# One decoder layer on one Trainium2 core: cell transposes placed later, gathered steps moved from the mixer to the dense pass, own rings for the attention's doubled halves

## Chip, cores and metric

The kernel runs on one core of one Trainium2 chip. The metric is the time of one execution on the device, in microseconds (us); each kernel is given by the median of its runs.

## What is computed

One layer of a hybrid decoder for 1024 tokens of width 1024 (batch 1), in float32. Cut to what matters:

```python
h = rms_norm(x); q, k, v, mq, mk, mv, mo, mi, mf = split(h @ w_in)
# group A: differential attention, 4 heads, two score maps of 64 columns each, ALiBi, causal
pr = softmax(q @ k.T * 64**-0.5 - slope * dist)            # for c in 0, 1
da = rms_norm((pr[0] - lam * pr[1]) @ v) * (1 - lambda_init)
# group B: mLSTM, 4 heads: causal conv and silu on mq and mk, a scan over chunks of 64 tokens
ml = rms_norm(sigmoid(mo) * mlstm_chunkwise(mq, mk, mv, mi, mf))
x += concat(da, ml) @ w_out
# PEER: 8 heads; per token and head the best 16 of 128 x 128 experts by product keys
q = (rms_norm(x) @ w_query).reshape(8, 2, 128)
eidx, g = top_k of the sums of the two halves' scores, softmax over the 16
x += sum_k g[k] * gelu(rms_norm(x) . expert_u[eidx[k]]) * expert_v[eidx[k]]
x += sigmoid(rms_norm(x) @ w_ple_gate) * (p @ w_ple_proj)
return rms_norm(x)
```

## The kernel before

**Stages.** `front(part)` runs for two parts of 512 tokens: the mixer (attention and mLSTM), the output projection (`wout`, eight weights), the query projection (`wq`, sixteen weights) and the choice of the experts. Then come `dense_up` and `dense_down` over 128 tables of the expert matrices each, and `tail` (the gate and the final norm) over eight tiles of 128 tokens. Every large product is done in three fp32r matmuls of high and low parts (`mm3s`), so each weight is loaded (`wraw`), copied to `whi` on ScalarE and subtracted to `wlo` on VectorE; a table likewise to `thi` (L841) and `tlo` (L842).

**Dense and gathered tiles.** Five of the eight token tiles go through all experts densely. The other three (tiles 0, 1, 2) gather their experts: `sparse` yields 400 steps, and a step gathers (but for the first and last sixteen, which have one half of it) one row of `expert_u` per token (`ru`, GpSimd's indirect DMA at L788, used on VectorE at L804) and one row of `expert_v` (`rv`, used at L822, which adds to `ya`). When the last step of a tile is done, `ya` is stored, and `tail` loads it again; tile 2 is the last of the tail's order `TORD`. `pump(rate)` pulls steps: before each projection, each output weight and each query weight of part 1 by `F_RATE`, before each table of `dense_up` by `UP_RATE` (the first rate up to the table given as third number, the second from there), each group of four tables of `dense_down` by `DOWN_RATE`, and in the tail. The first fourteen or so pulls in part 1 are the second top-k. The gathered rows land in a ring of `NR` buffers.

**The order of the work.** The kernel is written as generators that are stepped in turn; a scheduler fixes the order on every engine when the kernel is built, by the order of the code, the tiles' rings and priorities (a pulled step is put 800 places ahead, and `anchor` and `behind` keep a gathered instruction behind the last weight's split). On the chip each engine works off its own list.

**A head of the mixer.** `qkv(h)` projects queries, keys and values (three pieces). It takes `qT` from PSUM (L371), and `queries` and `keys` call `doubled`, which copies each half of the partitions twice by SyncE's DMAs (L260), and from these copies form `qab` and `kab`, the high and low parts for the scores `S` (L411). In part 1 the keys of part 0 come back from `kt_s`. `attention(h)` has six pieces: five steps over its query tiles, and a last one with the norm's `ro` chain (`rsqrt`, L116 to L125, on VectorE, four numbers per partition), the copies of `by_tile` (L364, ScalarE), the output's transposes (L448, TensorE) and `mixed`. `ml_inputs(h)` and `mlstm(h)` project and run the cell; the cell's last piece transposes its output (L558). `qT`, `kT`, the doubled halves, the attention's output `osb` and others share a ring `t2` of eight buffers of 512 columns (`T2`). The mixed tiles go to `mx_s` and are loaded again at the end of the mixer (L584 to L590).

**Queues.** SyncE's queue (SPq) holds weights, tables, doubled halves and mixed tiles in one order; GpSimd issues the gathers.

## Time and profile before

| | us |
|---|---|
| median of three runs (3212.78 to 3213.87) | 3213.16 |
| the profiled execution | 3213.83 |
| its span in the trace | 3212.0 |
| TensorE (PE) busy | 2954.8 (92%) |
| VectorE (DVE) busy | 2521.5 (79%) |
| ScalarE (ACT) busy | 1160.2 (36%) |
| GpSimd (POOL) busy | 1013.0 (32%) |
| DMA | 829.53 MB, 258 GB/s in the mean |

The stages lie in the span like this: part 0 to 465 us, part 1's mixer to 860, its output and query projections to 950, its top-k to 1065, the dense up pass to 2170, the dense down pass to 3075, and the tail to 3212. The busy times are means over these stages; a stage is read by its own stretch. A row of the stretches gives the length, the busy time of each engine with the number of its instructions, TensorE's granted clock (1.00 is the full one), the mean busy share of the 16 DMA engines and their rate.

### The profile page before, as it was taken

The numbers are of one execution on the slowest core, as the hardware profiler recorded it, in microseconds if no ns is written. First come the engines' busy times: TensorE is split into PE (matmuls) and PEld (weight loads), VectorE is DVE, ScalarE is ACT, GpSimd is POOL, SyncE is SP. The second block draws the span as 40 slices with busy tenths as digits, with TensorE's granted clock in tenths as the row PEclk, the third lists the DMA queues.
The fourth block names the chain that finished last, engine by engine and source line by source line (L and its number), as shares of the span: only waits on it lengthen the run. The fifth ranks groups of instructions, "written<-read, shape, count | busy, mean of one in ns | idle before, by whom it ended". The sixth has DMA issues, their size and how long they took to land.

```text
span 3212.0 us, 44687 instructions
## 1 busy us (share of the span) xinstructions
PE 2954.8 (92%) x16367; PEld 2601.1 (81%) x16367; DVE 2521.5 (79%) x5381; ACT 1160.2 (36%) x1994; POOL 1013.0 (32%) x786
## 2 busy tenths in 40 slices
PE   7998889887579799999999999988989999999987
PEld 6776767676467799999999999977878888887866
DVE  5564689888889999978766667557878888888786
ACT  5664335554322232245343433322222222222233
POOL 0000000344541544412433334343333444442330
PEclk9998989998789899999999999989999999999999
DMA  5333433678874788876888878899989999998762
GB/s 163 96 107 108 143 120 95 232 234 274 323 264 147 290 317 313 284 262 244 329 314 299 293 278 311 313 343 343 327 316 337 334 334 331 334 327 286 265 209 92
DMA packets 317148, 829.53 MB, mean 258 GB/s; under 512 B 26240, under 2 KB 115200, under 8 KB 314368
## 3 DMA queue, kind: packets, MB, share of 16 engines
q0 software_dynamic: 112608, 410.04, 36.2%
q1 hardware_dynamic: 185888, 374.68, 33.8%
q10 hardware_dynamic: 18432, 41.95, 3.5%
q8 instruction: 128, 2.10, 0.3%
q14 instruction: 92, 0.75, 0.1%
HBM read 715.95 MB, written 102.24 MB: 255 GB/s over the span
## 4 chain that ended last, share of the span: by engine, by line
PE 53%; DVE 19%; issue 14%; DMA 8%; POOL 4%; ACT 2%; SPq 0%; POOLq 0%; DVEq 0%; ACTq 0%
PE A L143 16%; PE mm L143 10%; PE keep L143 6%; DVE ya L822 3%; PE S L143 3%; DVE ru L804 2%; DMA rv<-in_ev,eidx 2%; PE Y L135 2%; PE Y L134 2%; PE Y L136 2%; DMA raw<-in_vr 2%; POOL rv L788 2%; PE pg L894 2%; PE pg L895 2%; DVE tlo L842 2%
## 5 line engine op out<-in xcount | busy, mean ns | idle before, releaser
L788 POOL DMA_INDIRECT ru<-in_eu,eidx x384 | 507.5, 1321 | 1201.8 <-DVE ru L804 845.1
L788 POOL DMA_INDIRECT rv<-in_ev,eidx x384 | 497.5, 1296 | 442.6 <-DVE ya L822 300.7
L842 DVE TENSOR_TENSOR tlo<-raw,thi 128x1024 fp32r<-128x1024 f32 x256 | 312.9, 1222 | 299.1 <-issue 168.5
L822 DVE SCALAR_TENSOR_TENSOR ya<-rv,cf,ya 128x1024 f32<-128x1024 f32 x384 | 492.8, 1283 | 40.3 <-DMA rv<-in_ev,eidx 28.1
L841 ACT ACTIVATE thi<-raw 128x1024 fp32r<-128x1024 f32 x256 | 268.0, 1058 | 683.4 <-PE A L143 380.8
L804 DVE SCALAR_TENSOR_TENSOR ru<-ru,sh 128x1024 f32<-128x1024 f32 x384 | 468.8, 1221 | 20.8 <-DMA ru<-in_eu,eidx 19.6
L143 PE MATMUL A<-ahi,thi 128*128 128x384 f32 x1024 | 348.7, 341 | 4.3 <-ACT ga L954 4.3
L143 PE MATMUL A<-alo,thi 128*128 128x384 f32 x1024 | 346.6, 338 | 0.0
L143 PE MATMUL mm<-ahi,whi 128*128 128x512 f32 (+1 forms) x752 | 299.7, 402 | 22.2 <-ACT ahi L234 12.4
L143 PE MATMUL mm<-alo,whi 128*128 128x512 f32 (+1 forms) x752 | 286.2, 393 | 7.1 <-DVE alo L235 7.1
L134 PE MATMUL Y<-thi,ph 128*128 128x512 f32 x640 | 250.3, 391 | 6.6 <-ACT thi L841 4.8
L143 PE MATMUL A<-xh,thi 128*128 128x256 f32 x1024 | 250.8, 283 | 0.7 <-ACT xh L933 0.7
L143 PE MATMUL A<-xl,thi 128*128 128x256 f32 x1024 | 250.6, 282 | 0.1
L135 PE MATMUL Y<-tlo,ph 128*128 128x512 f32 x640 | 249.8, 390 | 0.5 <-DVE tlo L842 0.5
L136 PE MATMUL Y<-thi,pl 128*128 128x512 f32 x640 | 249.5, 390 | 0.0
L143 PE MATMUL A<-ahi,tlo 128*128 128x384 f32 x1024 | 202.7, 338 | 13.8 <-DVE tlo L842 13.7
L1021 ACT ACTIVATE ph<-aq 128x640 fp32r<-128x640 f32 x128 | 87.5, 729 | 330.8 <-PE Y L135 325.3
L143 PEld LDWEIGHTS A<-ahi,thi 128*128 128x128 f32 x1024 | 195.1, 191 | 4.5 <-ACT ga L954 4.5
L143 PE MATMUL mm<-ahi,wlo 128*128 128x512 f32 (+1 forms) x752 | 193.7, 388 | 5.5 <-DVE wlo L194 5.5
L143 PEld LDWEIGHTS A<-xh,thi 128*128 128x128 f32 x1024 | 195.0, 190 | 1.0 <-ACT xh L933 0.9
L143 PEld LDWEIGHTS A<-xl,thi 128*128 128x128 f32 x1024 | 194.8, 190 | 0.3 <-DVE xl L934 0.3
L143 PEld LDWEIGHTS A<-alo,thi 128*128 128x128 f32 x1024 | 195.0, 190 | 0.0
(462 smaller groups left out, 6160.0 us busy)
## 6 DMA issues: line engine op xcount, KB each, us to landing
raw<-in_ut SPq DMA_DIRECT2D x128, 512.0 KB, 5.9
raw<-in_vr SPq DMA_DIRECT2D x128, 512.0 KB, 5.5
ga_s<-ga ACTq DMA_DIRECT2D x128, 320.0 KB, 5.6
g_s<-st SPq DMA_DIRECT2D x20, 2048.0 KB, 8.3
gq<-g_s SPq DMA_DIRECT2D x32, 1280.0 KB, 10.8
aq<-ga_s SPq DMA_DIRECT2D x32, 1280.0 KB, 8.7
wraw<-in_win SPq DMA_DIRECT2D x58, 512.0 KB, 3.4
wraw<-in_wq SPq DMA_DIRECT2D x32, 512.0 KB, 3.7
```

The costliest lines, as they stand in the source:

```text
L134: pe.matmul(o, lh, rh, start=start, stop=False)
L135: pe.matmul(o, lh, rl, start=False, stop=False)
L136: pe.matmul(o, ll, rh, start=False, stop=stop)
L143: pe.matmul(o, ll if p == "l" else lh, rl if p == "r" else rh, start=start and p == "h", stop=stop and n == last and p == names[-1])
L788: gp.indirect_dma_start(out=b, out_offset=None, in_=table, in_offset=bass.IndirectOffsetOnAxis(ap=eidx[part][:, i, k:k + 1], axis=0))
L804: behind(v.scalar_tensor_tensor(b, b, 1.0, st["h", tl], op0=OP.mult, op1=OP.mult, accum_out=st["d", n][:, j:j + 1]))
L822: op = v.scalar_tensor_tensor(ya, b, st["c", n][:, j:j + 1], ya, op0=OP.mult, op1=OP.add)
L841: sc.activation(hi, raw, AF.Copy)
L842: anchor(v.tensor_sub(lo, raw, hi.bitcast(F32)))
L894: pe.matmul(pg[:, b, :], o0[:, a, :, b], w0[:, a, :, b], start=True, stop=False)
L895: pe.matmul(pg[:, b, :], o0[:, a, :, b], w1[:, a, :, b], start=False, stop=True)
L1021: sc.activation(ph, av, AF.Copy)
```

## The change

The constants: `NR` 4 to 3 for the ring of gathered rows in the front, and a ring of its own with `NRU = 4` for `dense_up`; the doubled halves get a ring `dd` of two, `qT` and `kT` a ring `qk` of two, in place of `t2`, which stays at eight. The pump rates of the front fall, those of `dense_up` change, those of `dense_down` and the tail stay. In the mixer's loop the generators are stepped in another order; `attention` yields six times, so a seventh step of it does nothing.

```diff
-NR = 4
+NR = 3
+NRU = 4
+NDD = 2
...
-F_RATE = (2.4, 1.6, 2.0)
-UP_RATE = (1.0, 1.2, 56)
+F_RATE = (1.8, 1.3, 1.5)
+UP_RATE = (0.9, 1.45, 40)
 DOWN_RATE = 1.05
...
                 def doubled(src, c):
-                    d = pa.tile([P, T], F32, name="t2", bufs=T2)
+                    d = pa.tile([P, T], F32, name="dd", bufs=NDD)
...
-                    qT = pa.tile([P, T], F32, name="t2", bufs=T2)
+                    qT = pa.tile([P, T], F32, name="qk", bufs=2)
...
-                    kT = pa.tile([P, T], F32, name="t2", bufs=T2)
+                    kT = pa.tile([P, T], F32, name="qk", bufs=2)
...
                     att, inputs = attention(h), ml_inputs(h)
-                    step(att, cell)
-                    for _ in range(4):
+                    step(att)
+                    step(inputs, cell, att)
+                    for _ in range(3):
                         step(inputs, att)
-                    step(att)
                     cell = mlstm(h)
                     nxt = qkv(h + 1) if h + 1 < H else None
-                    for _ in range(3):
-                        step(cell, nxt)
+                    step(att, cell, nxt, cell, nxt, att, cell, nxt)
                 step(cell)
...
     front(0, ptk)
-    ring["pool"] = rstk.enter_context(pool("rg", side="right"))
+    fring = ExitStack()
+    ring["pool"] = fring.enter_context(pool("rg", side="right"))
     ring["bufs"] = NR
...
     fstk.close()
+    fring.close()
+    ring["pool"] = rstk.enter_context(pool("rgu", side="right"))
+    ring["bufs"] = NRU
     dense_up(ptk)
```

The line numbers of the changed kernel are two higher up to the mixer's loop, and one higher behind it up to `tail`. In the built order three places show the change.

VectorE in part 1, inside the `ro` chain of the last head's attention (`ro_h`, `ro_m` and `ro_u` are the chain's, `ru` and `rv` gathered rows). Before:

```order
L822 SCALAR_TENSOR_TENSOR ya<-rv,cf,ya 128x1024
L123 TENSOR_TENSOR ro_h<-ro_u 128x4
L804 SCALAR_TENSOR_TENSOR ru,dots<-ru,sh_5145 128x1024
L124 TENSOR_TENSOR ro_h<-ro_h,ro_m 128x4
L822 SCALAR_TENSOR_TENSOR ya<-rv,cf,ya 128x1024
L125 SCALAR_TENSOR_TENSOR ro_u<-ro_h,ro_u 128x4
L804 SCALAR_TENSOR_TENSOR ru,dots<-ru,sh_5145 128x1024
L123 TENSOR_TENSOR ro_h<-ro_u 128x4
L822 SCALAR_TENSOR_TENSOR ya<-rv,cf,ya 128x1024
L124 TENSOR_TENSOR ro_h<-ro_h,ro_m 128x4
L804 SCALAR_TENSOR_TENSOR ru,dots<-ru,sh_5145 128x1024
```

After:

```order
L823 SCALAR_TENSOR_TENSOR ya<-rv,cf,ya 128x1024
L125 TENSOR_TENSOR ro_h<-ro_u 128x4
L805 SCALAR_TENSOR_TENSOR ru,dots<-ru,sh_5364 128x1024
L126 TENSOR_TENSOR ro_h<-ro_h,ro_m 128x4
L823 SCALAR_TENSOR_TENSOR ya<-rv,cf,ya 128x1024
L127 SCALAR_TENSOR_TENSOR ro_u<-ro_h,ro_u 128x4
L125 TENSOR_TENSOR ro_h<-ro_u 128x4
L126 TENSOR_TENSOR ro_h<-ro_h,ro_m 128x4
L127 SCALAR_TENSOR_TENSOR ro_u<-ro_h,ro_u 128x4
L125 TENSOR_TENSOR ro_h<-ro_u 128x4
L126 TENSOR_TENSOR ro_h<-ro_h,ro_m 128x4
```

Gathered instructions stand between all steps of the chain before, and between the first steps only after; the chains of the two heads ahead of it hold fewer of them too, and there the eviction of the next head's `qT` lies inside the chain.

SyncE's queue in part 1, between the second and the third head (`t_...`, `qk` and `kt_s` are the sources of doubled halves, `wraw` a projection's weight, `mx_s` a mixed tile that is stored). Before:

```order
L376 DMA vv<-v_s 128x512
L190 DMA wraw<-in_win 128x1024
L356 DMA mx_s<-t_6102 128x512
L260 DMA t_6177<-t_6175 64x512 x2
L260 DMA t_6184<-t_6175 64x512 x2
L260 DMA t_6192<-kt_s 64x512 x2
L260 DMA t_6197<-kt_s 64x512 x2
L190 DMA wraw<-in_win 128x1024
L260 DMA t_6276<-t_6274 64x512 x2
L260 DMA t_6281<-t_6274 64x512 x2
L190 DMA wraw<-in_win 128x1024 x2
```

After:

```order
L378 DMA vv<-v_s 128x512
L262 DMA dd<-qk 64x512 x4
L192 DMA wraw<-in_win 128x1024
L262 DMA dd<-kt_s 64x512 x4
L358 DMA mx_s<-t_6057 128x512
L262 DMA dd<-qk 64x512 x4
L192 DMA wraw<-in_win 128x1024 x2
```

The queries' doubles come ahead of the store of the attention's output, a weight stands between them and the stored keys' doubles, and all doubles go through the two buffers `dd`.

TensorE in part 0, at the end of a projection in the second head (`mm` is a projection's product, `t_983` the cell's output). Before:

```order
L143 MATMUL mm<-alo,whi 128x512
L558 MATMUL tr<-ident,t_983 128x128
L143 MATMUL mm<-ahi,wlo 128x512
L558 MATMUL tr<-ident,t_983 128x128
L143 MATMUL mm<-ahi,wlo 128x512
L558 MATMUL tr<-ident,t_983 128x128
L143 MATMUL mm<-ahi,wlo 128x512
L558 MATMUL tr<-ident,t_983 128x128
L143 MATMUL mm<-ahi,wlo 128x512 x5
L411 MATMUL S<-kab,qab 128x256 x2
```

After:

```order
L145 MATMUL mm<-alo,whi 128x512
L145 MATMUL mm<-ahi,whi 128x512
L145 MATMUL mm<-alo,whi 128x512
L145 MATMUL mm<-ahi,wlo 128x512 x8
L560 MATMUL tr<-ident,t_983 128x128 x4
L413 MATMUL S<-kab,qab 128x256 x2
```

The cell's transposes stand behind the projection's last products in place of between them.

## Rows read from the trace of the kernel before

**Rows 1.** Stretches: length, busy time (instructions) by engine, clock, DMA share.

```profile
core 0: us, PE busy (x) PEld busy (x) DVE busy (x) ACT busy (x) POOL busy (x), PEclk, DMA share, GB/s
...
860.00:950.00 90.00, 71.39 (x368) 60.89 (x369) 69.83 (x109) 27.66 (x46) 38.97 (x31) 0.87 0.78 291
950.00:1065.00 115.00, 95.82 (x467) 77.80 (x465) 114.90 (x557) 26.32 (x44) 28.23 (x19) 0.94 0.48 158
1065.00:1300.00 235.00, 227.58 (x1508) 225.71 (x1509) 233.38 (x795) 68.05 (x109) 114.12 (x87) 0.97 0.81 305
1300.00:2170.00 870.00, 855.08 (x6005) 841.49 (x6004) 619.11 (x735) 341.10 (x464) 318.75 (x240) 0.99 0.84 300
2170.00:3075.00 905.00, 875.92 (x3808) 719.90 (x3808) 755.93 (x969) 218.01 (x272) 345.04 (x266) 0.98 0.93 320
```

**Rows 2.** Stretches: part 1's heads from transposes to transposes, and the mixer's end.

```profile
485.00:559.20 74.20, 66.77 (x362) 53.78 (x360) 71.24 (x303) 42.84 (x87) 0.00 (x0) 1.00 0.27 83
559.20:643.70 84.50, 67.91 (x375) 56.29 (x375) 72.13 (x174) 45.67 (x106) 30.56 (x25) 0.91 0.69 232
643.70:735.60 91.90, 72.24 (x375) 59.09 (x375) 81.38 (x158) 46.10 (x106) 44.73 (x35) 0.87 0.76 251
735.60:829.30 93.70, 68.39 (x355) 55.64 (x356) 83.00 (x157) 46.37 (x109) 47.14 (x39) 0.85 0.80 267
829.30:860.00 30.70, 14.06 (x74) 12.53 (x72) 22.88 (x53) 10.13 (x30) 18.29 (x17) 0.61 1.00 377
```

**Rows 3.** TensorE's waits from 465 to 1065 us, by line.

```profile
engine line waited for: us in total, times, longest us
PE tr L448 <- ACT t L364: 46.3, 4, 16.2
...
PE tr L558 <- ACT t L364: 11.8, 2, 11.6
```

**Rows 4.** Costliest groups of the page: VectorE's two gathered instructions (busy, mean ns).

```profile
L822 DVE SCALAR_TENSOR_TENSOR ya<-rv,cf,ya 128x1024 f32<-128x1024 f32 x384 | 492.8, 1283 | 40.3 <-DMA rv<-in_ev,eidx 28.1
...
L804 DVE SCALAR_TENSOR_TENSOR ru<-ru,sh 128x1024 f32<-128x1024 f32 x384 | 468.8, 1221 | 20.8 <-DMA ru<-in_eu,eidx 19.6
```

**Rows 5.** Timeline of VectorE, up pass: two table splits, 33 tables apart (start, us).

```profile
1094.01 1.23 DVE L842 TENSOR_TENSOR tlo<-raw,thi 128x1024 fp32r<-128x1024 f32 x1
...
1337.83 1.22 DVE L842 TENSOR_TENSOR tlo<-raw,thi 128x1024 fp32r<-128x1024 f32 x1
```

**Rows 6.** Chain that ended last, up pass: three tables on TensorE (start, us).

```profile
1638.82 21.11 PE A L143 x144
```

**Rows 7.** Timelines of VectorE and TensorE, tail: gathered steps, last tile's transposes.

```profile
3080.37 1.28 DVE L822 SCALAR_TENSOR_TENSOR ya<-rv,cf,ya 128x1024 f32<-128x1024 f32 x1
...
3154.38 1.28 DVE L822 SCALAR_TENSOR_TENSOR ya<-rv,cf,ya 128x1024 f32<-128x1024 f32 x1 [1.24 <-DMA rv<-in_ev,eidx]
...
3185.49 0.60 PE L1101 MATMUL tr<-ident,x 128*128 128x128 f32 x4
```

**Rows 8.** Chain that ended last, from the second to the third head of part 1.

```profile
633.43 8.26 DMA ru<-in_eu,eidx
...
650.33 0.61 DVE t L371
...
655.60 9.74 DMA t<-kt_s
...
668.36 6.42 DMA t<-t
...
679.99 0.33 PE S L411
```

**Rows 9.** DMA issues, 1500 to 2000 us: median us from issue to landing.

```profile
rv<-in_ev,eidx POOLq DMA_INDIRECT x73, 6.3
```

**Rows 10.** DMA issues, 2400 to 2800 us.

```profile
rv<-in_ev,eidx POOLq DMA_INDIRECT x61, 8.2
```

## The prediction, on record before the changed kernel ran

> **What bounds the kernel now.** I read the stretches first [rows 1], because every stage has a different limit. In the dense passes (1300 to 3075 us) TensorE is busy 855.08 of 870 us and 875.92 of 905 us: nothing that happens on another engine can shorten these two by more than the rest, and a step put there costs nothing as long as it stays inside that engine's cover. In 950 to 1065 VectorE is busy 114.90 of 115 us, in 1065 to 1300 it is busy 233.38 of 235 us: there VectorE is the limit and every instruction taken from it counts, down to what TensorE needs. Before 950 no engine is full. There I read the heads of part 1's mixer one by one [rows 2]: cycles of 74.20, 84.50, 91.90 and 93.70 us, with 0, 25, 35 and 39 instructions on GpSimd, nearly all of them gathers. TensorE's busy time hardly grows (66.77 to 68.39 us), VectorE's grows from 71.24 to 83.00 us, and the granted clock goes from 1.00 to 0.85. So the heads are 47.5 us longer in sum than three times the one without gathers, for 99 gathers: 0.48 us each on average, and between the second and the fourth cycle (14 more gathers, 9.2 us) 0.66 us each. The waits of TensorE there [rows 3] say how: 46.3 us in four waits of the attention's transposes (L448), for the ACT copy that follows the `ro` chain on VectorE. That chain is a string of tiny instructions, and gathered steps of 1221 and 1283 ns [rows 4] stand between them.
>
> **The change, part by part.**
>
> *Steps of part 1.* The rates go from 2.4, 2.0, 1.6 to 1.8, 1.5, 1.3: 29 projections x 0.6 = 17.4, 8 output weights x 0.5 = 4, 16 query weights x 0.3 = 4.8, together 26.2 steps, each one `ru` and one `rv` instruction on VectorE, two issues on GpSimd and 1 MB from HBM. I counted in VectorE's order where they go missing (cumulative `ru` + `rv` at a landmark, before to after): at the last head's `ro` chain 80 to 63, so 17 fewer; at the mixer's closing copies (L590) 106 to 68, so 21 more gone; at the query projection's end 136 to 92, another 6.
>
> (a) Heads, to the last `ro` chain. 17 x 1.25 us = 21 us of VectorE time leaves. At 0.48 us each this gives 8 us. Another way: the new rate gives a head 7 x 1.8 = 12.6 steps, 25 gathers, as many as the cycle of 84.50 us had; so 91.90 and 93.70 would become about 84.5 (16.6 us), and the first 3 us less, 20 us. I take -15, bounds -8 to -21.
>
> (b) From there to L590. 21 instructions, 26 us of VectorE. The stretch 829.3 to 860 has VectorE at 22.88 of 30.70 us and the DMA engines full (1.00, 377 GB/s) [rows 2]; what stays is the last cell's own chain, whose transposes wait 11.6 us [rows 3], and the reload of the seven mixed tiles. I take -10, bounds -4 to -20.
>
> (c) 860 to 950. 6 instructions, 7.5 us, in a stretch where VectorE is busy 69.83 of 90 us and TensorE 71.39. I take -5, bounds 0 to -8.
>
> (d) 950 to 1065 holds the same VectorE work in both (21 gathered instructions and the second top-k): 0.
>
> *Steps of the dense up pass.* Rates 1.0 for 56 tables and 1.2 for 72 (142.4) become 0.9 for 40 and 1.45 for 88 (163.6): 21.2 more; the other 5 end up in the tail, since the down pass keeps its rate.
>
> (e) 1065 to 1300, VectorE's stretch. To table 41, VectorE's order has 33 fewer instructions than before, of which 17 are of earlier places; 16 x 1.29 = 20.7 us leave here. TensorE sets the floor: 33 tables took 1337.83 - 1094.01 = 243.8 us [rows 5], 7.39 us each, while three tables take 21.11 us, 7.04 each, where TensorE runs alone [rows 6]. 33 x 0.35 = 11.5 us can be had at most. I take -8, bounds 0 to -11.5.
>
> (f) 1300 to 2170 takes 25 steps more: 65 us of VectorE into 251 us idle, 26 MB more on 300 GB/s, so about 330 GB/s, which the down pass shows for the same engines (320 GB/s, share 0.93) with TensorE still at 97% [rows 1]. I take +2, bounds 0 to +20. The cover is TensorE's 855 us; a table's `thi` and `tlo` are two buffers deep, so a `tlo` that comes over 7 us late shows.
>
> (g) Down pass: same steps, 0.
>
> (h) Tail. Before, the last 18 `rv` instructions run from 3080.37 to 3154.38 us, 4.35 us apart [rows 7]; five more put the last at about 3176. Its tile is then stored and loaded again, some 6 us, and transposed: about 3182, where four of its eight transposes stood at 3185.49 anyway. I take +3, bounds 0 to +14.
>
> *Order of the mixer.* The attention's generator has six pieces, and its last one is already reached at the same place in both loops: TensorE's order shows the same neighbours for its transposes. Only the cell's transposes (L558) move, behind the first input projection of the next head. Their waits apart from the last of each part are about 1 us in all, and the last (11.6 us [rows 3]) isn't moved: 0.
>
> *Rings.* qT no longer waits for the ring slot of the attention's output. Before, L371 stands at 650.33 us, 6.6 us after the transposes start at 643.7, and from there the chain of waits runs through the doubling DMAs (9.74 us, then 6.42 us) to the first scores at 679.99 [rows 8]. In the new order L371 lies inside the `ro` chain; at most 6.6 us in each of three heads, 20 us. But the transposes on TensorE still wait for the same `ro` chain, now with L371 and one or two copies in it, and the second projection of the head follows behind them. I take -9, bounds +10 to -20. Against it, the gather ring has three buffers in place of four during the mixer: `ru` shows pieces of 8.26 us in the chain [rows 8], and with three a late landing reaches VectorE sooner. I take +6, bounds 0 to +14. In the dense pass there are four again.
>
> **The sum.** -15 -10 -5 +0 -8 +2 +0 +3 +0 -9 +6 = -36 us. The profiled execution has a span of 3212.0 and took 3213.83 us, 0.67 more than the median of the three runs shown (3213.16). 3213.16 - 36 = 3177 us. All bounds at their good ends give 3213 - 82 = 3131, at the bad ones 3213 + 46 = 3259.
>
> **The rivals.**
>
> *More comes back (about 3148).* The clock of 0.85 to 0.91 [rows 2] may rise again once the waits at L448 are short, and VectorE's time may come back one for one: (a) -21, (b) -20, (c) -8, (e) -11 and the queries -9, with +6, +2 and +3 against it, minus 58, with some 7 us of clock on top. For it: the cycle without gathers runs at clock 1.00. Against: the reload and the cell's chain are there in any case. TensorE's two levels are 1.2 and 2.4 GHz; in the rows the mean falls where it idles most, 0.61 where it was busy 14.06 of 30.70 us. The Trainium skill says the same in "TensorE: Matmul & The Clock Gate", section "HAM oscillation — how this bites in real kernels": idle stretches send the engine back to the lower level, and each return is paid again. By that rule these heads get faster on TensorE too, about the 7 us above; the trace agrees as far as the clocks fall with the idle time.
>
> *The dense pass pays (about 3190).* What leaves the mixer lands in a stage whose transfers already fill 0.84 of the engines. In the up pass a gathered `rv` lands 6.3 us after its issue [rows 9], in the down pass, at 0.93, 8.2 us [rows 10], and TensorE idles 3.2% there in place of 1.7%. If the up pass takes that idle share on: 870 x 1.5% = +13 in place of +2, and the sum is -25, or 3188 to 3190. For it: the gathers and the tables do slow each other in these rows. Against: 1.5% has causes of the down pass's own. The Trainium skill's "DMA: Bandwidth & Descriptors", section "Issuing engines are not separate DMA queues", states that transfers started by different engines run on the same 16 DMA engines and interleave, which speaks against this change: moved gathers are not separate from the table loads. The trace agrees with its 8.2 against 6.3 us.
>
> *No difference (3207 to 3219).* The reordering does nothing (in part certain: the attention's transposes stay where they were), the waits at L448 turn into waits of the same length for the doubling DMAs, and three buffers cost their 14 us: -8 -4 0 -4 +14 +3 +2, about 0.
>
> *Slower (about 3231).* One mechanism: two `dd` buffers. The doubles of qT, of the stored keys and of kT were eight deep and issued as fast as their sources came; now the keys' doubles must wait until qT's are consumed, kT's until the keys' are, in SP's queue, and the projection weights queue behind them. If qT's doubles are consumed no earlier than before, the path gets one serial round more per head: 9.74 us of transfer [rows 8] plus about 5 us of copies, 15 us in three heads, +45, against a gain elsewhere of -27 (without the queries' -9): +18, or 3231. For it: SP's order shows a weight load caught between these doubles, and such loads feed every projection. Against: in VectorE's order qT comes earlier, so the first round lies under the `ro` chain. It decides from the point at which the stored keys' doubles are issued later, after the head's transposes, than in the kernel before.
>
> **How the numbers follow.** Chances: forecast (3160 to 3190) 0.50; more comes back 0.17; the dense pass pays 0.12; no difference 0.10; slower 0.11. The predicted time is the forecast's. The range cuts the farther half of the high gain and nearly all of the slower case: 3146 to 3218, leaving out about 0.06 below and 0.12 above. A difference of 0.2% (6.4 us) is about what a measurement of this kernel can tell from no change: under 3206.7 is faster (0.50 + 0.17 + 0.12 = 0.79), within is 0.10, above 3219.6 is 0.11.
>
> **What would show each step right or wrong.** In the profile of the changed kernel: part 1's heads near 80 us each, with the waits of L448's successor below 30 us in sum, shows (a) and the rings; a start of the query projection 25 to 35 us earlier, (b); 33 tables in about 236 us, (e); TensorE still at 98% from there to the down pass, (f); the last tile's transposes not over 40 us from the end, (h). I am wrong if the doubles take the waits over (S L411 behind `kab` or `qab` for over 20 us in sum), if gathered instructions on VectorE wait for `ru` or `rv` in the mixer for over 20 us, or if the up pass loses over 10 us.

## The result, and the profile after

The changed kernel takes 3197.51 us (median of five runs, 3192.39 to 3203.47) beside 3213.54 us of the kernel before (3212.78 to 3216.08): a ratio of 0.9949, 95% interval 0.9934 to 0.9963. That is 16 us faster and clear of noise, inside the range of the prediction; the forecast was 36 us faster. A ratio, here and below, is estimated from all runs of both kernels and can differ from the quotient of the medians beside it by up to 0.001. The profiled execution has a span of 3198.5 us.

The first lines of its page: busy time of each engine and instructions.

```profile
span 3198.5 us, 44681 instructions
...
PE 2958.2 (92%) x16367; PEld 2601.9 (81%) x16367; DVE 2526.4 (79%) x5381; ACT 1157.9 (36%) x1992; POOL 1019.9 (32%) x786
```

The sums are those of before, to within 7 us: the change moves waiting, not work. Where the time went is read from marks that both programs share, taken from the timelines (start, us; the heads are part 1's; "the last scaling" is the fourth `dg` of L631, behind which the query projection's matmuls run):

| mark | before | after | difference |
|---|---|---|---|
| attention transposes, head 2 | 643.7 | 640.2 | -3.5 |
| head 3 | 735.9 | 733.4 | -2.5 |
| head 4 | 828.1 | 815.1 | -12.9 |
| the mixer's last closing copy (L590) | 868.9 | 846.0 | -22.9 |
| last scaling ahead of the query projection | 933.0 | 906.0 | -27.0 |
| first table split of the up pass | 1064.0 | 1037.2 | -26.8 |
| 128th table split | 2120.0 | 2105.9 | -14.1 |
| first split of the down pass | 2139.6 | 2125.7 | -13.9 |
| last split of the down pass | 3036.8 | 3020.1 | -16.8 |
| end | 3212.0 | 3198.5 | -13.5 |

So 27 us are gained up to the experts' choice, 13 are lost in the up pass, 3 gained in the down pass and 3 lost in the tail.

The heads in the stretches of the changed kernel, to be laid beside [rows 2] (same columns):

```profile
558.80:640.20 81.40, 67.11 (x375) 56.01 (x375) 70.07 (x169) 46.21 (x108) 23.67 (x21) 0.92 0.64 211
640.20:733.40 93.20, 73.24 (x375) 60.50 (x375) 77.12 (x151) 47.42 (x109) 38.32 (x30) 0.85 0.75 241
733.40:815.10 81.70, 66.85 (x351) 55.71 (x351) 62.62 (x131) 42.06 (x100) 31.73 (x24) 0.88 0.58 191
815.10:846.00 30.90, 21.33 (x101) 17.91 (x102) 11.00 (x37) 14.32 (x39) 0.30 (x1) 0.66 0.58 201
```

The second of these cycles has five gathers fewer than before and is 1 us longer. TensorE's waits in the mixer of the changed kernel say the same: beside [rows 3] the first line has lost 3.8 us and the second 4.7.

```profile
PE tr L450 <- ACT t L366: 42.5, 4, 15.6
...
PE tr L560 <- ACT t L366: 7.1, 2, 6.8
```

What holds that cycle is seen in VectorE's timeline, inside the `ro` chain of the third head (the bracket is VectorE's idle time and what ended it):

```profile
723.43 0.16 DVE L126 TENSOR_TENSOR ro_h<-ro_h,ro_m 128x4 f32<-128x4 f32 x1
727.42 0.69 DVE L279 TENSOR_TENSOR qab<-dd,qab 64x512 fp32r<-64x512 f32 x1 [3.83 <-ACT qab L277]
728.14 0.16 DVE L127 SCALAR_TENSOR_TENSOR ro_u<-ro_h,ro_u 128x4 f32<-128x4 f32 x1
729.72 0.68 DVE L279 TENSOR_TENSOR qab<-dd,qab 64x512 fp32r<-64x512 f32 x1 [1.41 <-ACT qab L277]
```

The copies of the next head's queries now stand in the chain. They follow a ScalarE copy that follows a doubling DMA, and while VectorE waits for them (3.83 and 1.41 us) the chain waits too.

The up pass gains up to its 41st table split and loses behind it. In each pair the first row is the stretch up to that split and the second the rest up to the 128th. Before:

```profile
1064.00:1357.76 293.76, 285.34 (x1905) 283.47 (x1906) 289.97 (x916) 82.69 (x133) 138.37 (x107) 0.98 0.83 306
1357.76:2120.00 762.24, 761.93 (x5443) 752.99 (x5442) 532.71 (x579) 317.11 (x426) 267.37 (x199) 1.00 0.82 293
```

After:

```profile
1037.20:1326.00 288.80, 282.12 (x1888) 280.07 (x1887) 276.65 (x891) 81.38 (x131) 114.60 (x90) 0.98 0.80 281
1326.00:2105.90 779.90, 767.37 (x5473) 758.19 (x5472) 591.79 (x655) 318.82 (x430) 338.57 (x251) 0.99 0.87 322
```

So 5 us are gained and then 17.7 lost, and one stall of TensorE makes up most of the loss. The gate's block (L895) waits 12.5 us for VectorE in the stretch from 1490 to 1642 us:

```profile
PE pg L895 <- DVE w L886: 12.5, 1, 12.5
```

and VectorE's timeline ahead of it shows why: gathered rows that have not landed, a new tile's first row that waits for the tile's input (`sh`), and only then `w`, which the gate's block waits for.

```profile
1511.25 1.28 DVE L823 SCALAR_TENSOR_TENSOR ya<-rv,cf,ya 128x1024 f32<-128x1024 f32 x1 [3.54 <-DMA rv<-in_ev,eidx]
...
1521.86 1.23 DVE L805 SCALAR_TENSOR_TENSOR ru<-ru,sh 128x1024 f32<-128x1024 f32 x1 [1.25 <-DMA sh<-h_s]
...
1533.78 1.28 DVE L823 SCALAR_TENSOR_TENSOR ya<-rv,cf,ya 128x1024 f32<-128x1024 f32 x1 [2.50 <-DMA rv<-in_ev,eidx]
1534.98 0.55 DVE L869 CAST it<-pt 128x384 f16<-128x384 f32 x1
...
1540.19 1.22 DVE L886 TENSOR_TENSOR w<-o,it 128x2048 f16<-128x2048 f16 x1
```

The 40 us ahead of this block, before:

```profile
1516.80:1556.80 40.00, 40.00 (x281) 39.71 (x280) 29.89 (x36) 13.56 (x20) 24.00 (x19) 1.00 1.01 401
DVE ya L822 <- DMA rv<-in_ev,eidx: 1.5, 1, 1.5
```

After:

```profile
1501.50:1541.50 40.00, 27.50 (x189) 27.15 (x188) 26.16 (x34) 6.89 (x12) 23.01 (x19) 0.89 0.98 383
DVE ya L823 <- DMA rv<-in_ev,eidx: 10.3, 4, 3.5
```

The DMA engines are full in both (1.01 and 0.98) and GpSimd has 19 instructions in both, but VectorE waits 10.3 us for `rv` in place of 1.5. Why the rows come late there is not shown.

### The profile page after: what moved, and what is told of

It is laid out like the page before. It is cut to its first block, busy times and chain, and to the rows that moved or that the text cites. A ratio compares the mean times of both kernels' runs of the same rounds, so it can differ in the third digit from the quotient of the medians.

```text
span 3198.5 us, 44681 instructions
## 1 busy us (share of the span) xinstructions
PE 2958.2 (92%) x16367; PEld 2601.9 (81%) x16367; DVE 2526.4 (79%) x5381; ACT 1157.9 (36%) x1992; POOL 1019.9 (32%) x786
## 4 chain that ended last, share of the span: by engine, by line
PE 24%; DVE 10%; DMA 9%; issue 7%; POOL 1%; ACT 1%; SPq 0%; DVEq 0%; POOLq 0%; ACTq 0%
PE A L145 14%; DMA raw<-in_vr 5%; PE keep L145 3%; DVE ya L823 2%; DMA rv<-in_ev,eidx 2%; DVE aq L1021 2%; DVE tlo L843 2%; PE pg L895 1%; PE pg L896 1%; DVE ru L805 1%; DVE yac L1042 1%; PE Y L137 1%; PE Y L138 1%; PE Y L136 1%; ACT thi L842 1%
## 5 line engine op out<-in xcount | busy, mean ns | idle before, releaser
L789 POOL DMA_INDIRECT rv<-in_ev,eidx x384 | 504.8, 1315 | 455.1 <-DVE ya L823 310.3
L145 PE MATMUL A<-ahi,thi 128*128 128x384 f32 x1024 | 349.0, 341 | 16.8 <-ACT thi L842 13.8
```

Of the source, the lines that this page charges most:

```text
L145: pe.matmul(o, ll if p == "l" else lh, rl if p == "r" else rh, start=start and p == "h", stop=stop and n == last and p == names[-1])
L789: gp.indirect_dma_start(out=b, out_offset=None, in_=table, in_offset=bass.IndirectOffsetOnAxis(ap=eidx[part][:, i, k:k + 1], axis=0))
```

## The experiments

They ran in five groups, on several chips, on which the kernel before took 3208 to 3218 us. So ratios to before, measured in the same group, are compared, not times.

### The changed kernel once more

No edit.

> The changed kernel once more, as the mark beside which the other three of this group are read, since its five times spread over 11 us (3192.4 to 3203.5) where those of before spread over 3. If the spread comes from the chip, the median stays at 3197 +- 5 and the stall of 12.5 us on TensorE behind the gate block's split (in the up pass, at 1529 us of the first profile) is there in this profile too. If that stall comes and goes, it is what spreads the times: a profile without it should show a span near 3187.

Measured: 3192.68 beside 3208.49 us, ratio 0.9942 (0.9929 to 0.9955). The stall is there again, 11.6 us. The spread of the times is not explained by it; in the up pass only the first eight tables differ by much between the two profiles of this program (64.9 and 59.4 us), and why they do stays open. So the stretch up to the 41st split takes 283.9 us here, 10 less than before, and the rest 779.8 (779.9 in the first profile).

### The queries' copies behind the chain

```diff
 def queries(src, h):
...
-                        sc.activation(qab[:, c, 1, :], d, AF.Copy)
+                        first = sc.activation(qab[:, c, 1, :], d, AF.Copy)
+                        if "scaled" in st:
+                            tc.add_manual_dep(first.ins, st["scaled"],
+                                              mybir.DependencyInfo(mybir.DependencyClass.NoSync,
+                                                                   mybir.DependencyReason.SCHED_ONLY),
+                                              reason="behind the norm")
```

`st["scaled"]` is the last of the scaled copies of the previous head's output (L366).

> The changed kernel with one order added: the first copy of the next head's doubled queries (ScalarE, L277) is put behind the scaled copies of the attention's output. Theory: in the changed kernel the VectorE half of that copy stands inside the ro chain and waits for the doubling DMA (3.8 and 1.4 us in the third head of part 1), which gave back what fewer gathers had gained; moved out, the wait of the transposes there falls from 15.6 to about 10 us and the time by 4 to 7 us against the changed kernel. Rival: the copies are on the path to the next scores anyway; then the wait moves from the transposes to the scores S and the time stays within 2 us.

Measured: ratio 0.9923 (0.9904 to 0.9941), 6 us less than the changed kernel of the same group (3186.48 and 3192.68 us). The intervals overlap, so the times alone don't show a gain. The marks of the traces: the third head's transposes stand at 731.3 in place of 735.7 us, the fourth's at 808.9 in place of 815.8. The start of the up pass stands at 1031.9 us, where three executions with the early copies (the two above and that of the next experiment) have it at 1035.4 to 1037.9. The size is near what was expected, the way isn't. The wait of the third head's transposes didn't fall:

```profile
731.32 1.06 PE L456 MATMUL tr<-ident,t 128*128 128x128 f32 x3 [16.05 <-ACT t L371]
```

It was 16.31 us in the repeat of the changed kernel. Without the copies the chain holds more gathered instructions, and VectorE waits for gathered rows there instead, 4.2 us in the 32 us up to the transposes:

```profile
DVE ya L829 <- DMA rv<-in_ev,eidx: 2.5, 2, 1.4
DVE ru L811 <- DMA ru<-in_eu,eidx: 1.7, 2, 0.9
```

The gain lies ahead of the chain: from the second head's transposes to TensorE's wait it is 72.2 in place of 75.8 us. So it is likely that the early copies cost some 3.5 to 6 us; that they do it by lengthening the chain is not shown: with them away, gathered rows lengthen it as much.

### Other rates in the up pass

```diff
-UP_RATE = (0.9, 1.45, 40)
+UP_RATE = (1.12, 1.48, 72)
```

> The changed kernel with the up pass's rates (1.12 to table 72, then 1.48) in place of (0.9 to table 40, then 1.45): the same 163 steps in that pass, but four gathered instructions fewer on VectorE just ahead of the second gate block. Theory: the stall of 12.5 us on TensorE there comes from that burst, with a new gathered tile in its midst; without it the time falls by 8 to 13 us against the changed kernel. Rival: the up pass is at the limit of its transfers (share 0.94 there) and pays about the same wherever the steps stand; then the time stays within 3 us and TensorE idles elsewhere in the pass.

Measured: ratio 0.9927 (0.9911 to 0.9942), 5.3 us less than the changed kernel of the same group. The intervals overlap; the trace shows what changed:

```profile
PE pg L895 <- DVE w L886: 4.7, 1, 4.7
```

The stall at the second gate block is 4.7 us, not 11.6. The steps moved forward cost something too: up to the 41st split the pass now takes 297.9 us in place of 283.9, and from there 762.7 in place of 779.8. The gain is smaller than expected, and of the expected kind.

### The rates alone

```diff
-F_RATE = (2.4, 1.6, 2.0)
-UP_RATE = (1.0, 1.2, 56)
+F_RATE = (1.8, 1.3, 1.5)
+UP_RATE = (0.9, 1.45, 40)
```

> The kernel before with the new rates of the front and the up pass alone; order and rings as before. Theory (the gain is the gathered steps that left the mixer): 24 to 30 us less by the end of the query projection, 12 us of it lost in the up pass again, 3197 +- 5 in all, as the changed kernel. Rival (queries' eviction ahead of the ro chain's end is worth 9 us, as forecast): 3204 to 3208.

Measured: ratio 0.991 (0.9897 to 0.9923), 27 us less than before, and 11 less than the whole change on the same chip. Neither theory held: the moved steps are worth more than the change, and the rest of the change costs. Up to the start of the up pass this kernel gains 34 us (1064.0 to 1030.2).

### The rings at the old rates

```diff
-NR = 4
+NR = 3
+NDD = 2
...
-                    d = pa.tile([P, T], F32, name="t2", bufs=T2)
+                    d = pa.tile([P, T], F32, name="dd", bufs=NDD)
...
-                    qT = pa.tile([P, T], F32, name="t2", bufs=T2)
+                    qT = pa.tile([P, T], F32, name="qk", bufs=2)
-                    kT = pa.tile([P, T], F32, name="t2", bufs=T2)
+                    kT = pa.tile([P, T], F32, name="qk", bufs=2)
```

> The kernel before with the own rings for doubled halves and for qT and kT and the gather ring of three; order and rates as before. The rates alone gave 27 us where the whole change gives 16, so something else costs about 11. Theory: the rings cost it, since with them the copies of the next head's queries come into the ro chain and wait there for their DMA: 5 to 10 us slower than before, and in the third head the copies' wait (4 to 5 us) stands inside the chain again. Rival of the prediction (the earlier eviction of qT gains 9, the ring of three costs 6): 0 to 5 us faster. Other rival (the order costs it): within 2 us of before.

Measured: ratio 1.0037 (1.0022 to 1.0052), 12 us slower. As the theory has it, the copies of the next head's queries stand in the third head's `ro` chain here too, and in the traces of the order alone and of the ring of three alone they don't:

```profile
723.91 0.69 DVE L278 TENSOR_TENSOR qab<-dd,qab 64x512 fp32r<-64x512 f32 x1 [4.52 <-ACT qab L276]
```

That they are what costs is answered by the ring of three alone, below.

### The order alone

The edit is the loop of the mixer as in the change, and nothing else.

> The kernel before with the new order of the mixer's steps alone; rings and rates as before. The prediction prices it at 0, since of the two transposes only the cell's move: within 3 us of before. Rival (the order costs what the rates' gain lost): 5 to 11 us slower.

Measured: ratio 0.9988 (0.9978 to 0.9997), 2.5 us less, at the edge of what can be told. The order costs nothing.

### Three buffers for the gathered rows alone

```diff
-NR = 4
+NR = 3
```

> The kernel before with three buffers in place of four for the gathered rows (front and up pass); the rest as before. The prediction prices it at +6 in the mixer, bounds 0 to 14; in the up pass, where TensorE hides VectorE's waits, nothing. Rival: a shallower ring keeps gathered steps from running ahead into the ro chains (five in place of seven in the second head's), and the time is 0 to 5 us shorter.

Measured: ratio 1.0042 (1.0031 to 1.0053), 13 us slower, as much as all rings together. So at the old rates the ring of three is the whole cost, and the rings for the doubled halves, with the copies that they draw into the chain, cost nothing that can be seen beside intervals of 7 and 10 us. Waits of VectorE from 860 to 1065 us, where before has none for gathered rows:

```profile
DVE ru L804 <- DMA ru<-in_eu,eidx: 5.7, 4, 4.0
...
DVE ya L822 <- DMA rv<-in_ev,eidx: 0.7, 2, 0.5
```

Three steps' worth slip as well: at the last head's transposes VectorE has done 85 gathered instructions in place of 91, and the end of the mixer gets them. In this run the up pass has the ring of three too; the changed kernel has four there. By the marks (of two chips) 5 us of the loss lie ahead of the up pass (first table split at 1069.2 in place of 1064.0 us) and 4 in it (1059.9 in place of 1056.0).

### Rates alone, with the other rates of the up pass

```diff
-F_RATE = (2.4, 1.6, 2.0)
-UP_RATE = (1.0, 1.2, 56)
+F_RATE = (1.8, 1.3, 1.5)
+UP_RATE = (1.12, 1.48, 72)
```

> The kernel before with the new rates of the front and, in the up pass, 1.12 to table 72 and 1.48 from there. Rates alone gave 3181.4 beside 3208.5 of before, with a stall of 12.2 us on TensorE behind the second gate block, and these up rates cut that stall from 11.6 to 4.7 us with the other rings. Theory: 5 to 8 us less than the rates alone, 32 to 35 us below before, the best of all so far. Rival: the stall is made up for later in the passes, whose transfers are near their limit, and the time is within 3 us of the rates alone.

Measured: ratio 0.9889 (0.9872 to 0.9907), 33 us less than before. The stall is 5.1 in place of 12.2 us, and the up pass takes 1057.1 in place of 1062.3. The intervals of this run and of the rates alone (0.9897 to 0.9923) overlap.

### Rates and order

The edit is the one above and the loop of the mixer as in the change.

> The kernel before with the new rates of the front, the up pass's rates 1.12 to table 72 and 1.48 from there, and the new order of the mixer's steps; the rings as before. If the parts add (33 us for the rates, 2.5 for the order), the ratio to before is 0.988 to 0.989, about 36 us less, the best so far. If the order's 2.5 us was chance, the same as the rates alone, 0.989 to 0.990.

Measured: ratio 0.9884 (0.9866 to 0.9901), 3174.73 beside 3211.01 us.

### More steps moved

```diff
-F_RATE = (1.8, 1.3, 1.5)
-UP_RATE = (1.12, 1.48, 72)
+F_RATE = (1.2, 1.0, 1.0)
+UP_RATE = (1.3, 1.71, 72)
```

> The kernel above with about 25 more steps moved from the front to the up pass (front 1.2, 1.0, 1.0; up pass 1.3 to table 72, then 1.71). Theory (heads short of gathered steps run at TensorE's pace, and the up pass has VectorE time left): another 10 to 20 us less by the start of the up pass, since no gathered instruction is left in the ro chains. Rival (the dense pass pays): the up pass, whose DMA share was 0.91 to 0.94 with 163 steps, is then near 1.00, and TensorE's idle time there grows from about 25 us by 10 or more, which leaves 0 to 5 us or a loss.

Measured: ratio 0.9819 (0.9804 to 0.9833), 3153.46 us, 57.5 us less than before, the fastest of all. The start of the up pass comes 46 us earlier than in the kernel above (981.8 and 1027.7), more than the theory gave; the up pass takes 13.5 us longer, as the rival said, though at a mean DMA share of 0.88 and not near 1.00. Another 13 us go between the 128th split and the last one (919.3 in place of 906.1 us, with as many gathers, 273 and 271); what takes them was not looked for. The waits at the attention's transposes (the second line) are down to 6.8 us in sum, from 46.3 before [rows 3]:

```profile
PE tr L558 <- ACT t L364: 6.8, 1, 6.8
PE tr L448 <- ACT t L364: 6.8, 4, 3.6
```

### Four buffers in the changed kernel

```diff
-NR = 3
+NR = 4
...
-T2 = 8
+T2 = 4
```

> The changed kernel with four buffers for the gathered rows in the front in place of three; the room comes from the ring t2, four buffers in place of eight, since the doubled halves, qT and kT have left it. Theory (the ring of three costs part of what the whole change lost against the rates alone): 4 to 8 us less than the changed kernel. Rival (the copies of the queries inside the ro chains cost all of it): within 3 us of the changed kernel. A shorter t2 may hold up the attention's and the cell's tiles; then it is slower, and the waits of VectorE for gathered rows would be short all the same.

Measured: ratio 1.005 (1.0036 to 1.0064), slower. The short `t2` holds up part 0 already, where nothing is gathered: its last head's transposes stand at 278.1 us, where the changed kernel has them at 264.0. So this run says nothing about the ring of gathered rows.

### The rates with the gather rings of the change

```diff
-NR = 4
+NR = 3
+NRU = 4
-F_RATE = (2.4, 1.6, 2.0)
-UP_RATE = (1.0, 1.2, 56)
+F_RATE = (1.8, 1.3, 1.5)
+UP_RATE = (0.9, 1.45, 40)
...
     fstk.close()
+    fring.close()
+    ring["pool"] = rstk.enter_context(pool("rgu", side="right"))
+    ring["bufs"] = NRU
```

> The kernel before with the changed kernel's rates and its gather rings (three in the front, four of its own from the up pass on), without the rings for the doubled halves and without the new order. Rates alone gave a ratio of 0.991, the whole change 0.994, and taking the copies out of the ro chains gave 0.992. Theory: the ring of three in the front costs what is left, about 4 to 6 us, seen as 5 us or more of waits of VectorE for gathered rows in the mixer over those of the rates alone: ratio 0.992 to 0.993. Rival: with fewer gathered steps the depth of the ring no longer matters in the front, the ratio stays at 0.991, and all of the loss lies with the doubled halves.

Measured: ratio 0.9924 (0.991 to 0.9937), as the theory has it; the intervals of this run and of the rates alone (0.9897 to 0.9923) overlap, so the 4.5 us are likely and not certain. The profiled execution took 3204.77 us, 12 above the median, so its marks are not used. VectorE's waits for gathered rows from 485 to 1065 us, with the rates alone:

```profile
DVE ru L804 <- DMA ru<-in_eu,eidx: 6.4, 5, 2.8
```

and with the ring of three:

```profile
DVE ru L805 <- DMA ru<-in_eu,eidx: 10.0, 8, 2.6
...
DVE ya L823 <- DMA rv<-in_ev,eidx: 2.0, 2, 1.8
```

### The chains freed, at the old and at the new rates

The number of steps is kept, and the gathered instructions are put behind the end of each `ro` chain: once on the kernel before, once (with 20 in place of 60) on the kernel with the new rates and order.

```diff
+    recent = []
+    NLATE = 60
...
+            recent.append(op.ins)
...
                     ro = rsqrt(pa, oss, NT, "ro", 1.0 / P)
+                    for late in recent[-NLATE:]:
+                        tc.add_manual_dep(late, wide[-1],
+                                          mybir.DependencyInfo(mybir.DependencyClass.NoSync,
+                                                               mybir.DependencyReason.SCHED_ONLY),
+                                          reason="behind the norm")
```

`recent` holds the gathered instructions of VectorE, and `wide[-1]` is the chain's last instruction.

> The kernel before, rates, rings and order as they were; only the last 60 gathered instructions pulled before a head's ro chain are ordered behind its end, so that none of them stands in a chain of part 1 (before: 7, 10 and 11). The number of steps in the mixer is the same. Theory (the place counts: every gathered instruction in the chain holds up TensorE's transposes): the waits at L448 fall from 46.3 to below 15 us, and 15 to 35 us are gained. Rival (the number counts, VectorE and the transfers are what is short in a head): the held instructions pile up behind the chain, the waits move to the next scores or to the cell's transposes, and the time is within 6 us of before, or longer.

Measured: ratio 1.0018 (1.0007 to 1.0028), 4.5 us slower. The waits at the transposes (L457 in this kernel) do fall, to 6.8 us in sum, and other waits take their place:

```profile
PE tr L567 <- issue: 22.1, 1, 22.1
PE S L415 <- ACT kab L271: 10.6, 3, 7.0
PE tr L457 <- ACT t L368: 6.8, 4, 3.6
```

Its stretches, from the second head of part 1 to the last scaling ahead of the query projection:

```profile
558.00:627.30 69.30, 67.78 (x374) 55.98 (x375) 51.59 (x135) 44.22 (x104) 9.92 (x8) 0.98 0.46 149
627.30:695.90 68.60, 66.98 (x376) 54.89 (x377) 43.98 (x103) 43.93 (x104) 0.00 (x0) 1.00 0.28 89
695.90:798.10 102.20, 73.48 (x352) 58.62 (x352) 80.81 (x162) 45.24 (x106) 45.30 (x34) 0.85 0.72 232
798.10:852.30 54.20, 23.61 (x89) 19.73 (x90) 51.35 (x93) 14.86 (x40) 40.41 (x36) 0.50 0.95 362
852.30:927.70 75.40, 52.82 (x224) 43.20 (x223) 68.00 (x104) 16.27 (x29) 47.12 (x37) 0.82 0.98 376
```

Two heads run almost without gathers, in 69 us each, and are 40 us ahead of before; then the held gathers come, and the next head and the mixer's end take 102 and 54 us. Of the 40 us, 17 are left at the mixer's last closing copy and 5 at the last scaling, and the first table split stands at 1069.9 us, 6 behind that of before. Where the held gathers come, VectorE (51.35 of 54.20 us, 68.00 of 75.40) and the DMA engines (0.95, 0.98) are both nearly full.

> The same hold (20 instructions suffice) on the kernel with the new rates of the front, 1.12 and 1.48 in the up pass, and the new order, which ran at a ratio of 0.988. One gathered instruction is left in the three chains, 22 before. Theory of the place: ratio 0.980 to 0.984, close to the kernel with 25 steps more moved (0.982). Rival (the number): 0.986 to 0.990.

Measured: ratio 0.9873 (0.9855 to 0.9891), beside 0.9884 without the hold: inside the rival's range again, and the intervals overlap. So the place inside the chain isn't worth the 14 us or more of the theory; the number of gathered instructions in the mixer costs, and the wait at the transposes is where it shows. The place may still be worth a few us at these rates: the fourth head's transposes stand 21.6 us earlier than without the hold (783.2 and 804.8) and the first table split 6.3 (1021.4 and 1027.7), but the last split of the down pass doesn't (2990.7 and 2990.1). What takes the rest in the passes was not looked for.

### Still more steps moved

```diff
-F_RATE = (1.2, 1.0, 1.0)
-UP_RATE = (1.3, 1.71, 72)
+F_RATE = (0.7, 0.6, 0.6)
+UP_RATE = (1.52, 1.88, 72)
```

> The kernel with 25 steps more moved (ratio 0.982) with another 20 moved to the up pass: front 0.7, 0.6, 0.6, up pass 1.52 to table 72, then 1.88. The chains were free already. If the place counted, little is left to gain in the mixer (up to 10 us, from the clock and the closing cell), and the up pass, which lost 14 us with the last step, loses 10 to 20 more: ratio 0.980 to 0.988. If the number counted, the mixer gains 20 us more and the ratio falls below 0.979.

Measured: ratio 0.9822 (0.9804 to 0.984), no better than with 20 steps fewer moved. The up pass starts 10 us earlier (971.8) and takes 15.6 us longer. The up pass of five kernels, first table split to 128th (columns as in [rows 1]; the gathers are the count in GpSimd's column): before, rates and order, the changed kernel, more moved, most moved.

```profile
1064.00:2120.00 1056.00, 1047.28 (x7345) 1036.46 (x7346) 822.67 (x1493) 399.80 (x559) 405.74 (x305) 0.99 0.82 297
```

```profile
1027.70:2084.00 1056.30, 1047.83 (x7359) 1036.37 (x7358) 863.51 (x1546) 399.76 (x560) 453.70 (x339) 1.00 0.85 314
```

```profile
1037.20:2105.90 1068.70, 1049.49 (x7359) 1038.27 (x7358) 868.45 (x1545) 400.20 (x560) 453.17 (x340) 0.99 0.85 311
```

```profile
981.80:2051.60 1069.80, 1048.12 (x7345) 1037.31 (x7346) 916.60 (x1620) 400.52 (x562) 514.96 (x386) 0.99 0.88 333
```

```profile
971.80:2057.20 1085.40, 1049.51 (x7345) 1038.79 (x7346) 962.64 (x1684) 402.21 (x563) 572.91 (x427) 0.98 0.90 347
```

The changed kernel's number of gathers, 339 or 340, costs 0.3 to 4.7 us in the four profiles with the rates 1.12 and 1.48 and 6.3 to 13.8 in the six with 0.9 and 1.45; 386 cost 13.8 us and 427 cost 29.4, while TensorE's work stays at 1047 to 1050 us. TensorE's waits at the gate's blocks grow with them; with 339 (rates and order), 386 and 427 gathers:

```profile
PE pg L893 <- DVE w L884: 4.3, 1, 4.3
...
PE pg L893 <- DVE w L884: 12.5, 2, 10.8
...
PE pg L893 <- DVE w L884: 22.3, 3, 15.4
```

The start of the up pass against the gathered instructions that VectorE has done by then gives the price of a gathered instruction ahead of the up pass: 157 at 1064.0 us (before), 113 at 1027.7 (rates and order), 64 at 981.8, 24 at 971.8. That is 0.8 us, 0.9 us and then 0.25 us for each. The count isn't all: the two kernels with the chains freed lie off this line, with 145 at 1069.9 us and 113 at 1021.4, by some 16 us and 6 us.

## Why the prediction was wrong

**The price of the steps was right.** (a), (b) and (c) without the rings come to -15 -10 -5 = -30; the rates alone gain 34 us up to there. The prediction's reading that gathered instructions are what lengthens a head stands, at 0.8 us each where it had taken 0.9 in the heads and 0.5 behind them. The freed chains show that most of this price doesn't hang on their place in the `ro` chain, as the prediction's text suggests. Whether it is VectorE's time or the transfers that come with each instruction is not separated: where the held gathers come, both are nearly full. The clock returns with the gathers' going, as the rival "more comes back" had it: 0.98 and 1.00 in the two heads without or nearly without gathers, 0.85 in the head that gets them all. The Trainium skill's "TensorE: Matmul & The Clock Gate", section "HAM oscillation — how this bites in real kernels", says that waits between groups of matmuls send the engine back to its lower clock; these three clocks agree.

**(f) failed most: the steps moved into the dense pass were priced at +2 and cost 17.7.** From the first table split to the 128th the sum had -8 +2 = -6; measured is +12.7, and +7.7 in the second profile. Parted at the 41st split, (e) is -5 and -10 in the two profiles, about its -8, and (f) is +17.7 and +17.5 in place of +2, within its bound of +20. The value was taken from mean idle time and mean rates, with TensorE's time as the cover. The loss is mostly not in the mean; it is one stall of 12.5 us (11.6 in the second profile) where a burst of gathered rows and a new tile stood ahead of a gate block on VectorE. The same number of steps laid otherwise costs 0.3 to 4.7 us. Here the rival "the dense pass pays" was right on the sum, not on the mechanism: the DMA share rose only from 0.82 to 0.85, and in the 40 us ahead of that block it was as high before, 1.01, without a stall. The Trainium skill's "DMA: Bandwidth & Descriptors", section "Issuing engines are not separate DMA queues", says that transfers which different engines start run on the same 16 DMA engines and interleave; no run here takes that apart, and 34 gathers more lengthened the pass by 0.3 us where they lay well.

**In the rings, qT's earlier eviction had the wrong sign.** The step took -9 for it and +6 for the ring of three. The +6 was about right: ahead of the up pass the ring of three costs some 5 us at the old rates by the marks, and likely 4.5 at the new ones. The -9 didn't come. At the old rates the other rings show no effect beside the ring of three. At the new ones the changed kernel starts the up pass at 1037.2 and 1037.9 us and the rates alone at 1030.2, so rings and order cost 7 to 8 us there, in place of -3; less the ring of three that is about +3 in place of -9. The earlier eviction draws the queries' copies forward, into the chain, where they wait for their DMA; the text names these copies ("now with L371 and one or two copies in it"), gives the bound of +10, and still takes -9. With them moved out the kernel is likely 3.5 to 6 us faster; by which wait they cost stays open.

**The sum.** In the profiled execution the parts are -26.8 up to the first table split, where the sum had -33, then -5.0, +17.7, -2.6 in the down pass and +3.2 behind it: -13.5 in place of -36. Of the prediction's signs of being wrong, the scores behind `kab` wait 0.7 us and VectorE waits 10.7 us for gathered rows in the mixer, both under the 20 named; the loss of over 10 us in the up pass came in the first profile. The waits at the attention's transposes were to fall below 30 us and are 42.5.

**The rest.** (d) was 0 and is 0 (131.0 and 131.2 us from the last scaling to the first table split). What the prediction calls the query projection's end, with 136 and 92 gathered instructions done, is this scaling: the query projection's matmuls start there, at 932.5 us before. (g) was 0 and is -3. (h) was +3 and is +3. The order was priced at 0 and gained 2.5 us alone, at the edge of what can be told. The rival of two `dd` buffers, with +18, is refuted by the rings at the old rates, which cost no more than the ring of three among them. The good ends of the bounds add up to -80.5, not -82, which moves 3131 to 3133 and nothing else.

## What to carry to other kernels

Price work that fills gaps on an in-order engine by its count in the stage, from two stretches with different counts, and not by the wait at which it shows: here, at the old rates, a hold that emptied the critical chain only moved the wait. A buffer that is freed earlier lets the scheduler pull its consumers forward, so ask which engine's queue they land in and what they wait for there. When work is moved into a stage that seems to have room, look for the places where that stage needs the engine at once (a gate block, a new tile), since its mean idle time doesn't tell of them; and when a move pays, move on until the receiving stage loses as much, which here gave 57 us where the change had taken 16.

## What was not expected of the hardware

Three buffers in place of four for transfers that land 6 to 8 us after their issue [rows 9, 10] cost 13 us of 3213, though each transfer is used by an instruction of 1.2 us. VectorE's waits for gathered rows grow from 9 to 21 us between 480 and 1065 us and from 2 to 13 in the up pass; the marks of the profiled execution show 5 and 4 us of it. And executions of one program differ by more than most of the effects read here: by 11 us for the changed kernel (3192.39 to 3203.47), and for the kernel before by 3 us in the first measurement but by 14 us in 24 executions of a later group (3204.42 to 3218.19); which waits make the difference was not found.
